# Tiles 64 bytes further on: where TensorE's two operands lie in a transformer block

## The chip, the cores and the metric

One core of a Trainium2 chip runs the whole program. The metric is the device time of one execution in microseconds (us); the figure for a kernel is the median of its runs.

## The reference

The kernel computes one block over 256 tokens of width 2048 in float32: a wide input projection, two branches (a gated delta rule with short convolutions, and a sparse attention that picks 64 keys per query), a gated merge, and a feed-forward part of width 5632, with two layer norms. Cut to its large products:

```python
proj = x @ w_in[l]                                   # 2048 -> 11864 columns
...
merged = jax.nn.sigmoid(gate_a) * (o_a @ w_branch_a[l]) + jax.nn.sigmoid(gate_b) * (o_b @ w_branch_b[l])
x = layer_norm(DEEPNORM_ALPHA * x + merged @ w_out[l], ln1_g[l], ln1_b[l])
h_gate, h_up = jnp.split(x @ w_ffn_in[l], 2, axis=-1)
x = layer_norm(DEEPNORM_ALPHA * x + (jax.nn.silu(h_gate) * h_up) @ w_ffn_out[l], ln2_g[l], ln2_b[l])
```

## The kernel before

Every large product is made of three products in TensorE's float32r type: each factor is split into a part that this type holds (`hi`) and the rest (`lo`), and hi·hi, hi·lo and lo·hi are summed in PSUM.

Weights come in chunks of 128 × 1024 float32. The helper `chunk` (L65) takes a buffer `raw`, loads it by a DMA from the SP queue, casts it on ScalarE into `hi` (L72) and subtracts on VectorE into `lo` (L74). `raw`, `hi` and `lo` lie in the pool `wp`, which has four buffers of each; consecutive chunks use them in turn.

Two helpers then multiply. In `group_ws` (L123) the weights are the stationary operand, those that lie still in TensorE, and the activations move: for each of four blocks of 128 rows and each of two blocks of 128 columns, the hi block meets 512 columns of an `X2` tile (both parts of the activations, side by side; L134), and the lo block meets 256 columns, their hi part alone (L136). Such a pair of matmuls is the unit of the text. 62 groups of 4 chunks of 8 pairs make 1984 pairs: 20 groups (640 pairs) in the first stage, up to about 293 us, and 42 (1344 pairs) for the feed-forward input, from 788 to 1264 us. In `xs_mm` (L146) it is the other way round: an activation block of 128 × 128 is the stationary operand and the weight chunk moves, 512 columns a matmul, three matmuls for hi·hi (L153), lo (L154) and the activations' lo part (L155). The activations are `X2` in the projections to gates and values, in `wo` and in the first feed-forward block, `oh_` and `ol_` in the two branch products, and `hH`/`hL` in the last product. In `block_xs_stag` four chunks of a block are kept in an extra pool (`ex`), not in `wp`.

`ws_mm` (L107), of the first block, has weights stationary and 256 columns moving; it is called for the four column blocks of `win` chunks and once more for the small weights in `oh_`/`ol_` (L117, L119, L120).

The order of TensorE and SP is that of the program text (`manual_schedule`); smaller products of the two branches are slipped in between chunks by `tick()`.

**Where the tiles lie.** A partition is filled from the left in the order of the pools: `cst`, `wp`, `sm`, then the tiles of the first phase (`p1`), which later give way to `x1`, `hH`, `hL` and the extra pools; `X2` lies at the right end, behind it only the small tile `pad`. Every tile starts on a multiple of 32 bytes. The starts in bytes of a partition, before the change:

| tile | start | start modulo 256 |
|---|---|---|
| `raw`, 4 buffers | 17024 + 4096 i | 128 |
| `hi`, 4 buffers | 33408 + 4096 i | 128 |
| `lo`, 4 buffers | 49792 + 4096 i | 128 |
| `warm` and the other small tiles (`sm`) | 66176 | |
| first tile of `p1`, later `x1` | 66624 | 64 |
| `hH`, `hL` | 83008 and on, steps of 4096 | 64 |
| `oh_`, `ol_` | 156736, 164928 | 64 |
| `hi`, `lo` of the extra pools | 140352 and on | 64 |
| `X2`, 4 tiles | 196480 + 8192 i | 128 |

A stationary block takes 512 bytes of a partition, and blocks follow each other at multiples of 512 bytes; a moving operand of 512 columns takes 2048 bytes.

Of the kernel before, what the change touches and what calls it, by code (L numbers as in the profile page):

```python
# [8 lines left out]
F32 = mybir.dt.float32  # L9
F32R = mybir.dt.float32r  # L10
# [7 lines left out]
P = 128  # L18
# [14 lines left out]
LEAD = 70  # L33
LN1_AHEAD = ((20, 20, 20), (38, 32, 22))
X1T_WAIT = (4, 5)
INV_WAIT = 6
VT_WAIT = 6
N_WARM = 9

C_ID, C_TRI, C_ONE, C_M1, C_M2, C_M3, C_LV, C_SH = 0, 128, 256, 384, 512, 640, 768, 960  # L40
# [4 lines left out]
def block_kernel(ctx: ExitStack, tc: tile.TileContext, xT, x, cpack, onehot, relb, convw, alog, dtb, gnw,  # L45
                 ws, wws, win, wba, wbb, wo, wfi, wfg, wfo, ln1g, ln1b, ln2g, ln2b, out):
    nc = tc.nc

    cst = ctx.enter_context(tc.tile_pool(name="cst", bufs=1, side="left"))
    wp = ctx.enter_context(tc.tile_pool(name="wp", bufs=4, side="left"))  # L50
    sm = ctx.enter_context(tc.tile_pool(name="sm", bufs=1, side="left"))
# [4 lines left out]
    def ps_aux():  # L56
        return aux.tile([P, 512], F32, name="aux", tag="aux")

    def ps_acc():
        return acc.tile([P, 512], F32, name="acc", tag="acc")  # L60
# [1 line left out]
    ident = cst.tile([P, P], F32, name="ident")  # L62
    ctx.enter_context(tc.manual_schedule(engines={mybir.EngineType.PE, mybir.EngineType.SP}))

    def chunk(src, pool=None, lead=LEAD):  # L65
        n = src.shape[1]
        pool = pool or wp
        with tc.high_priority(offset=lead):
            raw = wp.tile([P, n], F32, name="raw", tag="raw")
            nc.sync.dma_start(raw, src)  # L70
            hi = pool.tile([P, n], F32R, name="hi", tag="hi")
            nc.scalar.copy(hi, raw)  # L72
            lo = pool.tile([P, n], F32R, name="lo", tag="lo")
            nc.vector.tensor_sub(lo, raw, hi.bitcast(F32))  # L74
        return hi, lo

# [7 lines left out]
    def tick():  # L84
        clock[0] += 1
        for ch in list(chains):
            wait = ch[1]
            if isinstance(wait, str):
                if wait not in done or done[wait] >= clock[0]:
                    continue  # L90
            elif wait > clock[0]:
                continue
            try:
                n = next(ch[0])
            except StopIteration:
                chains.remove(ch)
                continue
            ch[1] = n if isinstance(n, str) else clock[0] + n
# [24 lines left out]
    def group_ws(srcs):  # L123

        pss = [ps_acc(), ps_acc()]
        for ci, src in enumerate(srcs):
            hi, lo = chunk(src)
            hv = hi.rearrange("p (k c) -> p k c", k=4)
            lv = lo.rearrange("p (k c) -> p k c", k=4)
            for kk in range(4):  # L130
                k = 4 * ci + kk
                for c in range(2):
                    cs = slice(c * P, (c + 1) * P)
                    nc.tensor.matmul(pss[c], hv[:, kk, cs], X2[k // 4][:, k % 4], start=(k == 0), stop=False,  # L134
                                     skip_group_check=True)
                    nc.tensor.matmul(pss[c][:, :S], lv[:, kk, cs], xh[:, k, :], start=False, stop=(k == KT - 1),  # L136
                                     skip_group_check=True)
            tick()
        return pss
# [17 lines left out]
    def block_xs(srcs, lh, ll):  # L157
        pss = [ps_acc(), ps_acc()]
        for ci, src in enumerate(srcs):
            hi, lo = chunk(src)  # L160
            for tb in range(NTB):
                xs_mm(pss[tb], hi, lo, ci, len(srcs), lh, ll, tb)
            tick()
        return pss

    def block_xs_stag(srcs, lh, ll, extra, after):

        pss = [ps_acc(), ps_acc()]
        n = len(srcs)
        held = []  # L170
        for ci, src in enumerate(srcs):
            hi, lo = chunk(src, extra if n - 8 <= ci < n - 4 else None)
            xs_mm(pss[0], hi, lo, ci, n, lh, ll, 0)
            if ci < n - 8:
                xs_mm(pss[1], hi, lo, ci, n, lh, ll, 1)
            else:
                held.append((ci, hi, lo))
            tick()
        after(0, pss[0])
        for ci, hi, lo in held:  # L180
            xs_mm(pss[1], hi, lo, ci, n, lh, ll, 1)
            tick()
        after(1, pss[1])
# [8 lines left out]
    padp = ctx.enter_context(tc.tile_pool(name="padp", bufs=1, side="right"))  # L192
    pad = padp.tile([P, 24], F32, name="pad")
    nc.vector.memset(pad, 0.0)
    xs_ = ExitStack()
    xpool = xs_.enter_context(tc.tile_pool(name="xp", bufs=1, side="right"))
    X2 = [xpool.tile([P, KT // 4, 2, S], F32R, name=f"X2_{i}") for i in range(4)]
# [58 lines left out]
    def groups(chain, ev, *args):  # L256

        for c in (0, 2):
            b = gidx[0]
            gidx[0] += 1  # L260
            start(chain(c, group_ws([wws[b, k] for k in range(4)]), ev if c else None, *args))
# [22 lines left out]
    a = ps_aux()  # L284
    for _ in range(N_WARM):
        nc.tensor.matmul(a[:, :P], s_bm[:, 0, :P], s_bm[:, 0, P:], start=True, stop=True)
# [3 lines left out]
    for i in range(8):  # L290
        k0 = 2 * i
        parts = [srcs[i]] if i > 2 else [srcs[i][:, :512], srcs[i][:, 512:]]
        for j, src in enumerate(parts):
            k, n = k0 + j, 2 // len(parts)
# [3 lines left out]
            hi, lo = chunk(src, lead=0)  # L298
# [289 lines left out]
    def value_chain():  # L588
        for h0, ev in ((0, "vc0"), (4, "vc1")):
            yield ev  # L590
            yield VT_WAIT
            for tb in range(NTB):
# [368 lines left out]
    for f in range(2, FT):  # L961
        start(f_chain(f, group_ws([wfg[f - 2, k] for k in range(4)])))
# [115 lines left out]
```

## Time and profile before

| | us |
|---|---|
| median of 3 runs | 1511.9 |
| the runs | 1511.41, 1511.9, 1519.5 |
| the profiled execution, its own time | 1518.93 |
| its span, first to last instruction | 1517.2 |
| TensorE (PE) matmuls busy | 1502.1 (99%) |
| weight loads (PEld) busy | 1277.3 (84%) |
| VectorE (DVE) busy | 904.8 (60%) |
| ScalarE (ACT) busy | 696.1 (46%) |

PE is TensorE's matmuls and PEld its weight loads, which run beside them. A matmul's busy time includes the time in which its results drain; the next one starts before that ends, so busy times of PE overlap, and the distance between starts is what adds up to the span.

### The profile page before, as it was taken

The numbers are of one execution on the slowest core, as the hardware profiler recorded it, in microseconds if no ns is written. First come the engines' busy times: TensorE is split into PE (matmuls) and PEld (weight loads), VectorE is DVE, ScalarE is ACT, GpSimd is POOL, SyncE is SP. The second block draws the span as 40 slices with busy tenths as digits, with TensorE's granted clock in tenths as the row PEclk, the third lists the DMA queues.
The fourth block names the chain that finished last, engine by engine and source line by source line (L and its number), as shares of the span: only waits on it lengthen the run. The fifth ranks groups of instructions, "written<-read, shape, count | busy, mean of one in ns | idle before, by whom it ended". The sixth has DMA issues, their size and how long they took to land.

```text
span 1517.2 us, 20367 instructions
## 1 busy us (share of the span) xinstructions
PE 1502.1 (99%) x7920; PEld 1277.3 (84%) x7920; DVE 904.8 (60%) x1237; ACT 696.1 (46%) x914; POOL 40.2 (3%) x40
## 2 busy tenths in 40 slices
PE   9999999999999999999999999999999999999997
PEld 8888888888888888888888888888888888888885
DVE  6798984465464554565675555555555555545455
ACT  6765443445544344443444444444444444333341
POOL 0011010020100000000000000000000000000000
PEclk9999999999999999999999999999999999999999
DMA  8646574434465555558545555555555556555562
GB/s 295 188 154 201 173 188 153 153 125 167 153 219 194 190 188 193 190 182 296 194 158 190 186 189 183 191 182 188 187 183 192 181 190 241 193 194 192 189 207 92
DMA packets 86352, 284.59 MB, mean 188 GB/s; under 512 B 15776, under 2 KB 16840, under 8 KB 85488
## 3 DMA queue, kind: packets, MB, share of 16 engines
q1 hardware_dynamic: 77856, 273.39, 54.6%
q0 software_dynamic: 1360, 7.54, 1.7%
q10 hardware_dynamic: 7040, 2.36, 0.7%
q8 instruction: 62, 1.02, 0.3%
q14 instruction: 34, 0.28, 0.0%
HBM read 280.44 MB, written 2.82 MB: 187 GB/s over the span
## 4 chain that ended last, share of the span: by engine, by line
PE 97%; DMA 1%; DVE 1%; ACT 0%; issue 0%; SPq 0%; POOLq 0%; DVEq 0%; ACTq 0%
PE acc L134 31%; PE acc L153 15%; PE acc L136 15%; PE acc L155 15%; PE acc L154 15%; PE aux L585 1%; DMA raw<-in_win_dram 1%; PE aux L800 0%; PE aux L739 0%; PE aux L479 0%; PE aux L454 0%; PE aux L566 0%; PE aux L499 0%; ACT hi L72 0%; PE aux L651 0%; DVE lo L74 0%
## 5 line engine op out<-in xcount | busy, mean ns | idle before, releaser
L74 DVE TENSOR_TENSOR lo<-raw,hi 128x1024 fp32r<-128x1024 f32 (+1 forms) x515 | 632.4, 1230 | 509.1 <-ACT hi L72 508.1
L72 ACT CAST hi<-raw 128x1024 fp32r<-128x1024 f32 (+1 forms) x515 | 538.2, 1046 | 654.1 <-PE acc L155 353.9
L134 PE MATMUL acc<-X,hi 128*128 128x512 f32 x1984 | 703.3, 399 | 0.0
L136 PE MATMUL acc<-X,lo 128*128 128x256 f32 x1984 | 556.1, 280 | 0.0
L134 PEld LDWEIGHTS acc<-X,hi 128*128 128x128 f32 x1984 | 372.7, 188 | 92.3 <-issue 1.0
L136 PEld LDWEIGHTS acc<-X,lo 128*128 128x128 f32 x1984 | 374.5, 189 | 0.0
L153 PE MATMUL acc<-hi,X 128*128 128x512 f32 x544 | 214.6, 394 | 0.0
L155 PE MATMUL acc<-hi,X 128*128 128x512 f32 x544 | 212.1, 390 | 0.0
L154 PE MATMUL acc<-lo,X 128*128 128x512 f32 x544 | 211.9, 390 | 0.0
L153 PE MATMUL acc<-hi,hH 128*128 128x512 f32 x352 | 138.7, 394 | 0.0
L155 PE MATMUL acc<-hi,hL 128*128 128x512 f32 x352 | 138.0, 392 | 0.0
L154 PE MATMUL acc<-lo,hH 128*128 128x512 f32 x352 | 136.6, 388 | 0.0
L155 PEld LDWEIGHTS acc<-hi,X 128*128 128x128 f32 x544 | 102.1, 188 | 21.6
L154 PEld LDWEIGHTS acc<-lo,X 128*128 128x128 f32 x544 | 102.2, 188 | 20.6
L153 PEld LDWEIGHTS acc<-hi,X 128*128 128x128 f32 x544 | 102.2, 188 | 20.6
L155 PEld LDWEIGHTS acc<-hi,hL 128*128 128x128 f32 x352 | 66.1, 188 | 15.4
L154 PEld LDWEIGHTS acc<-lo,hH 128*128 128x128 f32 x352 | 66.1, 188 | 14.7
L153 PEld LDWEIGHTS acc<-hi,hH 128*128 128x128 f32 x352 | 66.2, 188 | 13.2
L953 ACT COPY ft<-acc 128x256 f32<-128x256 f32 x84 | 31.0, 369 | 62.6 <-PE acc L136 62.6
L954 DVE TENSOR_TENSOR ft<-acc,ft 128x256 f32<-128x256 f32 x84 | 35.4, 421 | 26.7 <-ACT ft L953 26.7
L153 PE MATMUL acc<-hi,oh__102 128*128 128x512 f32 x128 | 50.7, 396 | 0.0
L154 PE MATMUL acc<-lo,oh__102 128*128 128x512 f32 x128 | 50.3, 393 | 0.0
(268 smaller groups left out, 864.0 us busy)
## 6 DMA issues: line engine op xcount, KB each, us to landing
raw<-in_wfg_dram SPq DMA_DIRECT2D x168, 512.0 KB, 3.3
raw<-in_win_dram SPq DMA_DIRECT2D x101, 512.0 KB, 3.3
raw<-in_wfo_dram SPq DMA_DIRECT2D x88, 512.0 KB, 3.3
raw<-in_wws_dram SPq DMA_DIRECT2D x80, 512.0 KB, 3.4
raw<-in_wo_dram SPq DMA_DIRECT2D x32, 512.0 KB, 4.4
raw<-in_wbb_dram SPq DMA_DIRECT2D x16, 512.0 KB, 3.3
raw<-in_wba_dram SPq DMA_DIRECT2D x16, 512.0 KB, 3.3
raw<-in_wfi_dram SPq DMA_DIRECT2D x8, 512.0 KB, 4.4
```

The lines of the kernel that those rows point to most:

```text
L72: nc.scalar.copy(hi, raw)
L74: nc.vector.tensor_sub(lo, raw, hi.bitcast(F32))
L134: nc.tensor.matmul(pss[c], hv[:, kk, cs], X2[k // 4][:, k % 4], start=(k == 0), stop=False, skip_group_check=True)
L136: nc.tensor.matmul(pss[c][:, :S], lv[:, kk, cs], xh[:, k, :], start=False, stop=(k == KT - 1), skip_group_check=True)
L153: nc.tensor.matmul(ps, xh, hv[:, kk], start=(k == 0), stop=False)
L154: nc.tensor.matmul(ps, xh, lv[:, kk], start=False, stop=False)
L155: nc.tensor.matmul(ps, xl, hv[:, kk], start=False, stop=(k == 2 * n - 1))
L585: nc.tensor.matmul(o, l, r, start=True, stop=True)
L953: nc.scalar.copy(t[:, i], ps[:, S:])
L954: nc.vector.tensor_add(t[:, i], ps[:, :S], t[:, i])
```

## The change

The hi and lo tiles of the pool `wp` grow by 32 elements (128 bytes). A chunk is put `at` elements into its tile: 16 (64 bytes) where `group_ws` asks for it, 0 elsewhere. A new tile `pads` of 64 bytes, set to zero and read by nobody, is the first of the pool `sm`, which follows `wp`.

```diff
+WS_AT = 16
...
-    def chunk(src, pool=None, lead=LEAD):
+    def chunk(src, pool=None, lead=LEAD, at=0):
...
             raw = wp.tile([P, n], F32, name="raw", tag="raw")
             nc.sync.dma_start(raw, src)
-            hi = pool.tile([P, n], F32R, name="hi", tag="hi")
+            hi = pool.tile([P, n + (2 * WS_AT if pool is wp else 0)], F32R, name="hi", tag="hi")[:, at:at + n]
             nc.scalar.copy(hi, raw)
-            lo = pool.tile([P, n], F32R, name="lo", tag="lo")
+            lo = pool.tile([P, n + (2 * WS_AT if pool is wp else 0)], F32R, name="lo", tag="lo")[:, at:at + n]
             nc.vector.tensor_sub(lo, raw, hi.bitcast(F32))
...
         for ci, src in enumerate(srcs):
-            hi, lo = chunk(src)
+            hi, lo = chunk(src, at=WS_AT)
...
     nc.vector.memset(pad, 0.0)
+    pads = sm.tile([P, 16], F32, name="pads")
+    nc.vector.memset(pads, 0.0)
```

The buffers of `hi` then start at 33408 + 4224 i and those of `lo` at 50304 + 4224 i, both at 128, 0, 128, 0 modulo 256; the weights of `group_ws` begin 64 bytes later, at 192, 64, 192, 64. All that lies behind `wp` on the left moves by 1024 + 64 = 1088 bytes: `hH`, `hL`, `oh_`, `ol_` and the extra pools' chunks then start at 128 modulo 256. `raw` and `X2` stay where they were.

## Rows read from the trace of the kernel before

**Rows 1.** The page's busy table, and the mean granted clock of the core.

```profile
PE 1502.1 (99%) x7920; PEld 1277.3 (84%) x7920; DVE 904.8 (60%) x1237; ACT 696.1 (46%) x914; POOL 40.2 (3%) x40
...
core 0: 1517.2 us, clock 0.998
```

**Rows 2.** The page's chain that ended last, by engine and by line.

```profile
PE 97%; DMA 1%; DVE 1%; ACT 0%; issue 0%; SPq 0%; POOLq 0%; DVEq 0%; ACTq 0%
PE acc L134 31%; PE acc L153 15%; PE acc L136 15%; PE acc L155 15%; PE acc L154 15%; PE aux L585 1%; DMA raw<-in_win_dram 1%; PE aux L800 0%; PE aux L739 0%; PE aux L479 0%; PE aux L454 0%; PE aux L566 0%; PE aux L499 0%; ACT hi L72 0%; PE aux L651 0%; DVE lo L74 0%
```

**Rows 3.** The page's groups: count, busy us, mean ns, idle before.

```profile
L74 DVE TENSOR_TENSOR lo<-raw,hi 128x1024 fp32r<-128x1024 f32 (+1 forms) x515 | 632.4, 1230 | 509.1 <-ACT hi L72 508.1
L72 ACT CAST hi<-raw 128x1024 fp32r<-128x1024 f32 (+1 forms) x515 | 538.2, 1046 | 654.1 <-PE acc L155 353.9
L134 PE MATMUL acc<-X,hi 128*128 128x512 f32 x1984 | 703.3, 399 | 0.0
L136 PE MATMUL acc<-X,lo 128*128 128x256 f32 x1984 | 556.1, 280 | 0.0
...
L153 PE MATMUL acc<-hi,X 128*128 128x512 f32 x544 | 214.6, 394 | 0.0
...
L153 PE MATMUL acc<-hi,hH 128*128 128x512 f32 x352 | 138.7, 394 | 0.0
...
L153 PE MATMUL acc<-hi,oh__102 128*128 128x512 f32 x128 | 50.7, 396 | 0.0
```

**Rows 4.** Windows, 787 to 1265 us: length, busy us (count) per engine, clock, DMA.

```profile
787.00:1265.00 478.00, 478.00 (x2704) 414.53 (x2703) 272.04 (x338) 227.66 (x339) 1.11 (x2) 1.00 0.57 188
```

**Rows 5.** Timeline (start us, us, engine, line), long stage: pairs 1 and 7.

```profile
899.94 0.40 PE L134 MATMUL acc<-X,hi 128*128 128x512 f32 x1
...
902.06 0.40 PE L134 MATMUL acc<-X,hi 128*128 128x512 f32 x1
```

**Rows 6.** Timeline of TensorE, first stage: pairs 1 and 13.

```profile
274.81 0.40 PE L134 MATMUL acc<-X,hi 128*128 128x512 f32 x1
...
278.97 0.40 PE L134 MATMUL acc<-X,hi 128*128 128x512 f32 x1
```

**Rows 7.** Timeline of TensorE, `ws_mm`: matmuls 1 and 13 of each run.

```profile
25.68 0.28 PE L117 MATMUL acc<-X,hi 128*128 128x256 f32 x1
...
27.12 0.28 PE L117 MATMUL acc<-X,hi 128*128 128x256 f32 x1
...
27.48 0.28 PE L117 MATMUL aux<-X,oh__102 128*128 128x256 f32 x1
...
28.84 0.28 PE L117 MATMUL acc<-X,hi 128*128 128x256 f32 x1
```

**Rows 8.** Timeline of TensorE, `xs_mm` over `X2`: matmuls 1 and 31.

```profile
450.11 0.39 PE L153 MATMUL acc<-hi,X 128*128 128x512 f32 x1
...
456.91 0.39 PE L153 MATMUL acc<-hi,X 128*128 128x512 f32 x1
```

**Rows 9.** Timeline of TensorE, `xs_mm` over `oh_`, `hH`: matmuls 1 and 31.

```profile
499.81 0.39 PE L153 MATMUL acc<-hi,oh__102 128*128 128x512 f32 x1
...
506.68 0.39 PE L153 MATMUL acc<-hi,oh__102 128*128 128x512 f32 x1
...
1300.27 0.39 PE L153 MATMUL acc<-hi,hH 128*128 128x512 f32 x1
...
1307.14 0.39 PE L153 MATMUL acc<-hi,hH 128*128 128x512 f32 x1
```

**Rows 10.** Timeline of TensorE, chunks in the extra pool: matmuls 1 and 10.

```profile
742.87 0.39 PE L153 MATMUL acc<-hi,X 128*128 128x512 f32 x1
...
744.97 0.39 PE L153 MATMUL acc<-hi,X 128*128 128x512 f32 x1
```

**Rows 11.** Start: `pad`'s memset (timeline), first chunk's load (chain).

```profile
0.80 0.08 DVE L194 MEMSET pad<- 128x24 f32 x1 [0.80 <-PEq L1068]
...
3.06 4.85 DMA raw<-in_win_dram
```

## The prediction

> **What bounds the kernel.** I read the busy shares first [rows 1]: TensorE is busy 99% of the span and its clock is at the 2.4 GHz level throughout (granted clock 0.998). The chain that ended last says the same: 97% of it is TensorE, and five matmul lines carry 91% [rows 2]. A change that moves no bytes and adds no matmul can only matter through the distance from one matmul's start to the next. That distance is not in the groups' means (394 to 399 ns for 512 columns [rows 3]): those include the drain, which overlaps the next matmul. I take it from start times in the timeline, over many matmuls at once.
>
> For the pairs of `group_ws` (512 columns under a hi weight block, then 256 under a lo block) six pairs take 902.06 − 899.94 = 2.12 us, 353.3 ns a pair [rows 5]; the whole stage of 42 groups agrees, as 42 × 32 = 1344 pairs fill about 475 of its 478 us [rows 4]. At the end of the first stage the same pair, at the same addresses, takes 4.16 / 12 = 346.7 ns [rows 6]: there are two rhythms, and a stage can hold either.
>
> Now the same shapes by where the operands lie. I write "distance" for the address of the weights being loaded for the next matmul minus that of the moving operand, modulo 256 bytes; it follows from the table of addresses, and every step inside a tile is a multiple of 512 bytes.
> - 256 columns, distance 0: 1.44 / 12 = 120.0 ns. Distance 192 (stationary operand 64 past a multiple of 128, moving operand on one): 1.36 / 12 = 113.3 ns [rows 7].
> - 512 columns, distance 0: 6.80 / 30 = 226.7 ns [rows 8]. Distance 192: 6.87 / 30 = 229.0 ns, both with `oh_` and with `hH` [rows 9]. Distance 64 (here the moving operand is the one off the multiple of 128): 2.10 / 9 = 233.3 ns [rows 10].
>
> So the placement of the two operands TensorE reads at one time does set its pace, by up to 7 ns a matmul. The short rhythm of a pair is just the two rows of distance 0 added, 226.7 + 120.0 = 346.7; the long one has 6.6 ns more.
>
> The Trainium skill speaks against all this: "TensorE: Matmul & The Clock Gate", section "Step-by-step: what each phase is for", says that weights are loaded through a read port of their own and take nothing from the running matmul, and "SBUF — State Buffer", section "SBUF: two separate sides", that TensorE waits for nobody. By the first page's warm gap (512 / 2.4 + 2.5) a 512-column matmul would be 215.8 ns wherever its operands lie, and the change would do nothing. The trace disagrees: 226.7, 229.0 and 233.3 ns at one shape and one clock.
>
> **The change, part by part.** The profiled execution took 1518.9 us, 7.0 above the median of 1511.9. That is about what 1344 pairs differ by between the two rhythms (6.6 × 1344 = 8.9 us; the three runs lie 8.1 apart), so I read it as a run whose long stage fell into the long rhythm.
>
> 1. *Weights 64 bytes into their tiles.* The moving X2 stays on a multiple of 128 and the weights are 64 past one. The rows nearest in kind (stationary off, moving on) are 113.3 ns for 256 columns and 229.0 for 512, together 342.3. In the long stage that saves 353.3 − 342.3 = 11.0 ns × 1344 = 14.8 us. In the first stage the 640 pairs lie between 346.7 and 353.3; I take 350, which saves 7.7 × 640 = 4.9 us. Bounds for the pair: nothing seen is under 113.3 + 226.7 = 340.0, and 120.0 + 233.3 + 6.6 = 360 has all that rows show against it.
> 2. *The 1088 bytes behind the weight buffers* (8 × 128 + 64). `hH`, `hL`, `oh_`, `ol_` go from 64 past a multiple of 128 onto one, so `xs_mm` meets the case of [rows 8]: 229.0 − 226.7 = 2.3 ns on 3 × (352 + 128) = 1440 matmuls [rows 3], less 48 whose chunks lie in the extra pool at distance 0 already, 3.2 us saved. The chunks kept in the extra pools move by 1088 as well: 233.3 − 226.7 = 6.6 ns on 96 matmuls (two staged blocks over X2, four chunks each), 0.6 us saved. The 48 matmuls of the small weights lose what they had, +6.7 ns, 0.3 us. Tiles of the chains move together and keep their distances to one another.
> 3. *The cast and the subtraction* write 64 bytes further on, same shape and count: 1046 and 1230 ns [rows 3]. No row shows such a write; between no cost and a tenth more (0.1 us of each) nothing shows, since a chunk of `group_ws` lasts 8 × 353 = 2.8 us and ACT and DVE stand idle 654 and 509 us before these very lines. Without that cover 248 chunks × 0.1 would be 25 us. The loads into `raw` keep their addresses.
> 4. *The new memset* is like that of `pad`, 0.08 us of DVE, while the first weight chunk is still to land (4.85 us from 3.06) [rows 11]; uncovered it would be 0.08 us.
>
> Sum: 1518.9 − 14.8 − 4.9 − 3.2 − 0.6 + 0.3 = 1495.7, say **1496 us**. It starts from the profiled execution, but each term replaces a pace by a pace, so it doesn't depend on which rhythm a run of before had. Were the new pair to have a long rhythm too, 6.6 × 1344 = 8.9 us come back: 1504.6.
>
> **The rivals.**
>
> *The pace goes by 256 bytes, and half the buffers land wrong.* The tiles grow by 128, so the four buffers of hi and lo alternate: their starts modulo 256 are 128, 0, 128, 0, and the shifted weights lie at distance 64, 192, 64, 192 from X2. For it: distances 64 and 192 differ in the trace (233.3 against 229.0), although they are the same modulo 128. Against it: those two also differ in which operand is off the multiple of 128, and distance 64 with the stationary one off is in no row. Then half the pairs are 342.3, the other half 233.3 + 113.3 to 126.6 = 346.6 to 359.9; mean about 347.8. The moving chunks of `xs_mm` alternate as well, and half of them are 128 from the stationary operand, which no row shows; I take 231.1, midway between 64 and 192 (bounds 226.7 and 233.3). Over X2 that is +4.4 ns × 768 = +3.4 us; over `hH` and `oh_` half gain 2.3 and half lose 2.1, about zero. Time: 1518.9 − 5.5 × 1344 / 1000 − 2.2 × 640 / 1000 + 3.4 − 0.6 + 0.3 = **1513 us** (1505 to 1521), no change that can be told.
>
> *Slower, by the same alternation at its dear end.* The place is `group_ws` in buffers 0 and 2. If a pair there takes 359.9 and the others carry the 6.6 ns of a long rhythm (348.9), the mean is 354.4; against the short rhythm that I read into the median that is 7.7 × 1344 = 10.3 us, and 4.4 × 640 = 2.8 us in the first stage. With 233.3 at distance 128, `xs_mm` adds 6.6 × 768 = 5.1 and, over `hH` and `oh_`, (4.3 − 2.3) × 720 = 1.4 us. Time: 1511.9 + 19.6 = **1531 us**. It decides from a mean pair over about 349 ns with distance 128 at 231 or dearer. For it: the rhythm of long stages is the long one in this profile. Against: it needs both the 256 rule and the top of each bound.
>
> *The change does nothing.* The pair may be held by something that the addresses don't move, and only part 2 remains: about **1508 us** in the profile's terms of a short rhythm (1511.9 − 3.6). For it: the individual starts wander (the two rhythms) at fixed addresses. Against: 113.3 against 120.0, next to each other, same shape [rows 7]. The skill's rule above ends here too, with 1511.9 by its own gap.
>
> **How the numbers follow.** The forecast 0.42, the 256 rule without net effect 0.33, nothing 0.10, slower 0.15. Half a per cent, 7.6 us, is about what a measurement of this kernel tells from no change. Faster (under 1504.3): 0.40 of the forecast and 0.05 of the second case, 0.45. Slower (over 1519.5): 0.15 and 0.04, 0.19. The rest, 0.36, is the same. The range starts below the forecast, with the pair at 340.0 (1984 × 2.3 = 4.6 us less, 1491, and a little for the first stage's mean, 1490), and reaches over the second case to 1521; beyond lies most of the slower case, some 0.15. The forecast's own range is 1490 to 1505.
>
> **What would show it.** Right: in the changed profile the starts of `group_ws` pairs lie 342 ns apart in every chunk, `xs_mm` over `hH` and `oh_` runs at 226.7 ns as over X2, and the counts, the casts and the loads are as before. The 256 rule: the pair's distance changes from chunk to chunk, every second one dearer, and `xs_mm` alternates as well. Nothing: 346.7 or 353.3 in all chunks. It goes wrong if distance 64 with the stationary operand off is dear, if 128 is dear, or if a new long rhythm holds the pair.

## The result: 1527.4 us, slower

| kernel | median us | its runs |
|---|---|---|
| before | 1511.66 | six, 1510.5 to 1520.29 |
| after | 1527.36 | six, 1526.88 to 1527.97 |

The ratio is 1.0074, 95% interval 1.0047 to 1.0101: slower by some 0.7%, where 1496 was forecast. The runs of before lie at two times, near 1510.5 and near 1519.5, with none between 1512.5 and 1518.2 in 29 runs on one chip; those of after lie at one.

The page after: busy table, chain, groups (columns as in [rows 1 to 3]).

```profile
PE 1510.6 (99%) x7920; PEld 1280.7 (84%) x7920; DVE 905.0 (59%) x1238; ACT 695.5 (46%) x914; POOL 40.2 (3%) x40
...
PE 97%; DMA 2%; DVE 0%; SPq 0%; issue 0%; ACT 0%; POOLq 0%; DVEq 0%; ACTq 0%
...
L76 DVE TENSOR_TENSOR lo<-raw,hi 128x1024 fp32r<-128x1024 f32 (+1 forms) x515 | 632.3, 1229 | 514.2 <-ACT hi L74 513.1
L74 ACT CAST hi<-raw 128x1024 fp32r<-128x1024 f32 (+1 forms) x515 | 536.7, 1043 | 660.3 <-PE acc L157 363.1
L136 PE MATMUL acc<-X,hi 128*128 128x512 f32 x1984 | 704.4, 398 | 0.0
L138 PE MATMUL acc<-X,lo 128*128 128x256 f32 x1984 | 558.6, 282 | 0.0
...
L155 PE MATMUL acc<-hi,X 128*128 128x512 f32 x544 | 215.9, 397 | 0.0
...
L155 PE MATMUL acc<-hi,hH 128*128 128x512 f32 x352 | 138.0, 392 | 0.0
```

Behind the loads of the start nothing moved but the pace of TensorE: its clock is as before (0.998), the chain is 97% TensorE again, the counts are the same, and cast and subtraction take 1043 and 1229 ns against 1046 and 1230 [rows 3]. The groups hide the loss: the hi matmuls of `xs_mm` over `X2` are a little dearer (397 against 394), over `hH` a little cheaper (392 against 394). It shows in the starts. (Two lines were added above: L134, L136 and L153 of before are L136, L138 and L155 here.)

Timeline of TensorE after: start us, us, engine, line.

```profile
797.08 0.39 PE L136 MATMUL acc<-X,hi 128*128 128x512 f32 x1
...
899.27 0.40 PE L136 MATMUL acc<-X,hi 128*128 128x512 f32 x1
...
901.39 0.40 PE L136 MATMUL acc<-X,hi 128*128 128x512 f32 x1
...
902.44 0.40 PE L136 MATMUL acc<-X,hi 128*128 128x512 f32 x1
...
904.21 0.40 PE L136 MATMUL acc<-X,hi 128*128 128x512 f32 x1
...
1302.04 0.39 PE L155 MATMUL acc<-hi,hH 128*128 128x512 f32 x1
...
1302.74 0.39 PE L155 MATMUL acc<-hi,hH 128*128 128x512 f32 x1
...
1304.78 0.40 PE L155 MATMUL acc<-hi,hH 128*128 128x512 f32 x1
...
1307.57 0.39 PE L155 MATMUL acc<-hi,hH 128*128 128x512 f32 x1
...
1310.30 0.40 PE L155 MATMUL acc<-hi,hH 128*128 128x512 f32 x1
```

- *Pairs.* In a chunk at distance 192 six pairs take 901.39 − 899.27 = 2.12 us, 353.3 ns each; in the next chunk, at 64, five take 1.77 us, 354 by these rounded starts. Both are at the pace of the long rhythm of before [rows 5]. No group of the long stage runs faster: with the change of place between chunks counted in, each pair takes 352.9.
- *`xs_mm`.* Of the last five rows, four are the starts of successive chunks of twelve matmuls, at distances 0, 128, 0 and 128 (1302.74 is the fourth matmul of the first): 2.74, 2.79 and 2.73 us. Once settled, nine matmuls at distance 0 take 2.04 us, 226.7 ns; at 128 the starts lie 229 and 237.5 ns apart in turn, 233.3. The first three matmuls of a chunk at 0 still come 0.70 us apart, not 0.68: changing places costs a little too. Before, all were at 229.0 [rows 9].
- *Where the time came from.* From start to start in the two profiled executions: first pair 1.4 us later (37.76 against 36.39; the other profiles gave 36.2 to 38.9), the first stage 262.1 against 260.4, from it to the long stage 497.23 against 491.96, the long stage 474.5 against 475.1, the last product 242.8 against 241.5. That is 1.4 + 1.7 + 5.3 − 0.6 + 1.3 = 9.1, and 1518.9 + 9.1 = 1528.0; the profiled execution took 1527.97. The 1.4 us are the loads of the start: the last one in the chain (start us, us; first after, then before) lands at 28.27 us, before at 26.96. That the change has a part in this isn't shown.

```profile
23.16 5.11 DMA raw<-in_win_dram
...
22.07 4.89 DMA raw<-in_win_dram
```

### The profile page after: what moved, and what is told of

Its sections match the earlier page's. It is cut to its first block, busy times and chain, and to the rows that moved or that the text cites. A ratio compares the mean times of both kernels' runs of the same rounds, so it can differ in the third digit from the quotient of the medians.

```text
span 1526.1 us, 20368 instructions
## 1 busy us (share of the span) xinstructions
PE 1510.6 (99%) x7920; PEld 1280.7 (84%) x7920; DVE 905.0 (59%) x1238; ACT 695.5 (46%) x914; POOL 40.2 (3%) x40
## 4 chain that ended last, share of the span: by engine, by line
PE 97%; DMA 2%; DVE 0%; SPq 0%; issue 0%; ACT 0%; POOLq 0%; DVEq 0%; ACTq 0%
PE acc L136 31%; PE acc L138 16%; PE acc L157 15%; PE acc L155 15%; PE acc L156 15%; PE aux L589 1%; DMA raw<-in_win_dram 1%; DMA cp<-in_cpack_dram 1%; PE aux L804 0%; PE aux L743 0%; PE aux L483 0%; PE aux L458 0%; PE aux L570 0%; PE aux L503 0%; PE aux L655 0%; PE aux L469 0%
## 5 line engine op out<-in xcount | busy, mean ns | idle before, releaser
L76 DVE TENSOR_TENSOR lo<-raw,hi 128x1024 fp32r<-128x1024 f32 (+1 forms) x515 | 632.3, 1229 | 514.2 <-ACT hi L74 513.1
L74 ACT CAST hi<-raw 128x1024 fp32r<-128x1024 f32 (+1 forms) x515 | 536.7, 1043 | 660.3 <-PE acc L157 363.1
L136 PE MATMUL acc<-X,hi 128*128 128x512 f32 x1984 | 704.4, 398 | 0.0
L138 PE MATMUL acc<-X,lo 128*128 128x256 f32 x1984 | 558.6, 282 | 0.0
L136 PEld LDWEIGHTS acc<-X,hi 128*128 128x128 f32 x1984 | 373.0, 188 | 90.6 <-issue 1.0
L138 PEld LDWEIGHTS acc<-X,lo 128*128 128x128 f32 x1984 | 373.0, 188 | 0.0
L155 PE MATMUL acc<-hi,X 128*128 128x512 f32 x544 | 215.9, 397 | 0.0
L155 PE MATMUL acc<-hi,hH 128*128 128x512 f32 x352 | 138.0, 392 | 0.0
L155 PEld LDWEIGHTS acc<-hi,X 128*128 128x128 f32 x544 | 102.2, 188 | 22.0
L155 PEld LDWEIGHTS acc<-hi,hH 128*128 128x128 f32 x352 | 66.1, 188 | 14.9
L155 PE MATMUL acc<-hi,oh__104 128*128 128x512 f32 x128 | 50.7, 396 | 0.0
L157 PE MATMUL acc<-hi,ol__105 128*128 128x512 f32 x128 | 50.3, 393 | 0.0
```

The source lines that it names most:

```text
L155: nc.tensor.matmul(ps, xh, hv[:, kk], start=(k == 0), stop=False)
L157: nc.tensor.matmul(ps, xl, hv[:, kk], start=False, stop=(k == 2 * n - 1))
```

## The experiments

I call (hi, lo) a *place*: by how much the hi and the lo weights of `group_ws` lie past the X2 tile, modulo 256 bytes. The 512 columns of a pair run beside the load of the lo weights, the 256 columns beside that of the next hi weights: in the kernel before, the hi matmul that starts at 902.06 us [rows 5] and the lo matmul that starts at 902.29 us each start with a load (timeline of the weight loads):

```profile
902.06 0.19 PEld L136 LDWEIGHTS acc<-X,lo 128*128 128x128 f32 x1
902.29 0.19 PEld L134 LDWEIGHTS acc<-X,hi 128*128 128x128 f32 x1
```

Before is (0, 0); after is (64, 64) and (192, 192) in turn. Each interval is for the ratio to runs of before on the same chip.

**1. The 64 bytes behind the buffers alone.**

```diff
 (against the kernel before)
+    pads = sm.tile([P, 16], F32, name="pads")
+    nc.vector.memset(pads, 0.0)
```

> Only the 64-byte tile: the tiles do not grow and no chunk is shifted, so hH, hL, oh_, ol_ and the extra pools' chunks move by 64 bytes, onto the same place modulo 256 as hi, lo and X2 (distance 0 everywhere). Theory A, that the pace of TensorE goes by the distance of its two operands modulo 256 bytes: xs_mm over hH and oh_ falls from 229.0 to 226.7 ns a matmul, the extra pools' chunks from 233.3 to 226.7, group_ws keeps 346.7 or 353.3; 3 to 4 us less than before in the same rhythm. Rival B, that moving the tiles behind the weight buffers is itself what costs: xs_mm or the chains get dearer, and the time goes up towards 1520 us even where group_ws is in its short rhythm.

Measured: 1516.26 us (1515.0 to 1518.38), ratio 0.9989 (0.9971 to 1.0006). Timeline, matmuls 1 and 31 over `hH`:

```profile
1300.01 0.39 PE L153 MATMUL acc<-hi,hH 128*128 128x512 f32 x1
...
1306.81 0.39 PE L153 MATMUL acc<-hi,hH 128*128 128x512 f32 x1
```

6.80 / 30 = 226.7 ns: `hH` off its 64 runs as X2 does. This part of the sum holds, where the moving chunks stay in place. The long stage ran at 353.2 ns a pair, so the time belongs beside the 1519.5 of before: about 3 us, as costed. All twelve runs lie at this one time, though the pairs stand at the place where before's have two.

**2. The larger tiles without the shift.**

```diff
 (against the changed kernel)
-            hi, lo = chunk(src, at=WS_AT)
+            hi, lo = chunk(src)
```

> The changed kernel with the shift of group_ws taken back (its chunks begin at 0): tiles still grow by 128, so the four buffers alternate between distance 0 and 128. Theory A: xs_mm is as in the changed kernel, 226.7 ns in every second chunk and 233.3 in the others, which holds some 8 to 10 us of the change's loss; group_ws has 346.7 to 353.3 at distance 0 and an unknown pace at 128. Between 1517 and 1528 us. Rival C, that the shifted weights of group_ws hold the whole loss: back to 1512 or less.

Measured: 1521.26 us (1520.18 to 1523.48), ratio 1.0023 (1.0005 to 1.0041). Timeline: the start of the long stage, then of three successive chunks of twelve matmuls over `hH`, at 0, 128 and 0:

```profile
794.67 0.40 PE L136 MATMUL acc<-X,hi 128*128 128x512 f32 x1
...
1295.21 0.39 PE L155 MATMUL acc<-hi,hH 128*128 128x512 f32 x1
...
1297.95 0.40 PE L155 MATMUL acc<-hi,hH 128*128 128x512 f32 x1
...
1300.74 0.39 PE L155 MATMUL acc<-hi,hH 128*128 128x512 f32 x1
```

`xs_mm` alternates as after: 232.6 ns a matmul at 128, 228.1 at 0, the change of place counted in (2.79 and 2.74 us a chunk). The long stage starts at 794.67 us, 5.9 later than in before's profile, with no 64-byte shift anywhere, and its pairs, at (0, 0) and (128, 128) in turn, take 349.6. So the growth alone brings the loss in `xs_mm`, and the shift adds 6.1 us, mostly by holding the long stage at 353 (474.5 us against 470.1 here).

**3 and 9. Tiles that grow by 256, so that all buffers agree.** Everything of `group_ws` at 192, or at 64; `xs_mm` at 0 in every chunk.

```diff
 (against the changed kernel; hi and lo alike)
-            hi = pool.tile([P, n + (2 * WS_AT if pool is wp else 0)], ...)
+            hi = pool.tile([P, n + (64 if pool is wp else 0)], ...)
...
-WS_AT = 16
+WS_AT = 48    # the run at 192; 16 in the run at 64
...
-    tab = T("tab", [H, 384])
+    tab = s_u.rearrange("p a d -> p (a d)")[:H, :384]
```

> The changed kernel with tiles that grow by 256 instead of 128, so that all buffers lie alike, and the shift of group_ws at 192 bytes: distance 192 in all pairs, distance 0 in all of xs_mm. (tab takes its room from s_u for this.) The forecast's step, that a pair is the sum of its two rows at distance 192 (113.3 and 229.0): 342.3 ns a pair, 1496 us. Theory A, by the changed kernel's odd buffers: 353.3 ns a pair, xs_mm at 226.7 ns everywhere; 1515 to 1517 us.

> As the changed kernel, but the weight tiles grow by 256 bytes instead of 128 (and the 384-column table lies in the space of a scratch tile to make room), so every buffer keeps its place by 256: group_ws stands at distance 64 in every chunk, xs_mm at distance 0 in every chunk. If the loss of the change is the half of xs_mm that it puts at distance 128, then xs_mm goes back to 226.7 to 227 ns, the stage of the 42 last groups stays at 353 ns a pair, its start falls back from 797.1 us to within 2 us of 789, and the time is 1515 to 1519.5 us. If the loss came from group_ws at 64 or 192 itself, or from the larger tiles, the time stays at 1524 to 1528 us.

Measured at 192: 1517.25 us, ratio 0.9992 (0.997 to 1.0015); four runs at 1512.0 to 1512.3, six at 1517.1 to 1518.1. At 64: 1518.26 us (1517.23 to 1519.01), ratio 0.9998 (0.9987 to 1.001). Timeline of the run at 192, pairs 1 and 15:

```profile
899.58 0.39 PE L136 MATMUL acc<-X,hi 128*128 128x512 f32 x1
...
904.46 0.39 PE L136 MATMUL acc<-X,hi 128*128 128x512 f32 x1
```

Timeline of the run at 64, the start of the long stage, then pairs 1 and 13 of a group:

```profile
790.71 0.40 PE L136 MATMUL acc<-X,hi 128*128 128x512 f32 x1
...
899.74 0.40 PE L136 MATMUL acc<-X,hi 128*128 128x512 f32 x1
...
903.98 0.40 PE L136 MATMUL acc<-X,hi 128*128 128x512 f32 x1
```

4.88 / 14 = 348.6 and 4.24 / 12 = 353.3: the forecast's 342.3 is at neither place. At 64 the stage starts 6.4 us earlier than after and the run is 9.1 us shorter, with the pairs alike. So the half of `xs_mm` at distance 128 is what parts these two kernels: from the first stage to the long one after takes 497.2 us against 490.9 here, in the last product 242.8 against 239.2, together 10.0 us. Against before, whose `hH` and `oh_` lie at 192, the same stretches lost 6.6 us.

**4. A map of places.** One execution; the tiles as above, another place for each group of the long stage and another distance for each block of `xs_mm`.

```diff
+            hi, lo = chunk(src, dh=dh, dl=dl)    # places of this group
```

> A map in one run. Tiles grow by 256 and each chunk is put where a table says. The 42 groups of the long stage go through all 16 pairs of distances (hi, lo) from 0, 64, 128, 192, then ten equal finer ones (16, 32, 48, 240, 224, 208, 8, 248, 96, 160), then the 16 again; the 26 blocks of xs_mm that block_xs makes go through distances from 0 to 252. Theory A: a matmul of 512 columns runs at 226.7, 233.3, 233.3 and 229.0 ns at 0, 64, 128 and 192; finer steps show whether the pace changes in jumps or evenly. If hi and lo act each on its own (the 512-column matmul by lo's distance, the 256-column one by hi's), lo at 0 with hi at 192 gives 226.7 + 113.3 = 340 ns a pair; if the pair is locked as a whole, it stays at 346.7 or 353.3 in all 16. The time as a whole says little: 1515 to 1530 us.

Pairs, ns, pairs 5 to 29 of a group; each place stood twice and gave the same within 0.3 (but (0, 0): 352.3 over the first 14 pairs of the stage, and 346.7 the second time):

| hi \ lo | 0 | 64 | 128 | 192 |
|---|---|---|---|---|
| 0 | 346.7 to 352.3 | 346.7 | 346.7 | 350.0 |
| 64 | 340.0 | 353.3 | 350.0 | 353.3 |
| 128 | 351.8 | 346.7 | 351.1 | 346.7 |
| 192 | 340.0 | 346.7 | 346.7 | 353.3 |

`xs_mm`, 512 columns: 226.7 at distance 0, 228.9 at 4, 232 to 234 at 8, 239.5 at 12, 236.7 at 16, 230.0 at 48, 233.3 at 64, 232.4 at 128, 228.9 at 192, 237.2 at 252. Timeline of the map, `xs_mm` at distance 12, matmuls 1 and 10, then a group at (64, 0), pairs 1 and 13 (L170 and L151 are the hi lines here):

```profile
524.78 0.40 PE L170 MATMUL acc<-hi,oh__104 128*128 128x512 f32 x1
...
526.94 0.40 PE L170 MATMUL acc<-hi,oh__104 128*128 128x512 f32 x1
...
846.19 0.39 PE L151 MATMUL acc<-X,hi 128*128 128x512 f32 x1
...
850.27 0.39 PE L151 MATMUL acc<-X,hi 128*128 128x512 f32 x1
```

2.16 / 9 = 240 ns and 4.08 / 12 = 340.0. The fastest places, (64, 0) and (192, 0), take what the two fastest rows of one shape add up to, 226.7 + 113.3. Hi and lo both at 64 or both at 192 are among the dearest here, and (64, 192) with them. Equal distances alone are not what costs: ten finer places with hi and lo at one distance, each once, gave 346.7 at 16, 32, 48, 96 and 224, 348.9 at 8, 350.0 at 160 and 208, 351.7 at 248 and 353.3 at 240. For `xs_mm` no distance tried is as good as 0.

**5 and 6. Hi alone, lo alone.**

```diff
 (against the kernel before, with `pads`; the run with lo alone does the same to lo)
-            hi = pool.tile([P, n], F32R, name="hi", tag="hi")
+            hi = pool.tile([P, n + (4 * WS_AT if pool is wp else 0)], F32R, name="hi", tag="hi")[:, at:at + n]
```

> The changed kernel with the hi tiles alone grown, by 256, and the hi chunks of group_ws alone shifted, by 64; lo keeps its place, so that all of lo and all of xs_mm lie at distance 0. Theory A in the form that the map gave it: a matmul's pace goes by the distance of the weights that are loaded while it runs, those of the next matmul, so the 512-column matmul goes by lo (0: 226.7) and the 256-column one by hi (64: 113.3). 340.0 ns in every pair, 13.3 us... per thousand pairs less than the long rhythm of before; 1518.9 - 17.9 (long stage) - 6.4 (first stage) - 3.8 (xs_mm) = 1491 us, without two rhythms. Rival D, that the pace goes by the place of a matmul's own weights: the 512-column matmul has the shifted block (233), the 256-column one is at 120, 353 ns a pair, 1515 us.

> The same the other way round: lo alone grown by 256 and shifted by 64. Theory A: the 512-column matmul, which loads lo, gets dearer (229 to 231), the 256-column one stays near 117; 346.7 ns a pair as the map has it for hi 0, lo 64; 1518.9 - 8.9 - 2.1 - 3.8 = 1504 us. Rival D, own weights: 226.7 + 113.3 = 340 ns, 1491 us.

Measured, hi alone: 1510.3 us (1509.45 to 1512.15), ratio 0.9956 (0.9937 to 0.9974). Lo alone: 1505.48 us (1504.88 to 1506.18), ratio 0.9923 (0.9892 to 0.9954). Timeline with hi alone, pairs 1 and 13 in the first and in the long stage:

```profile
61.23 0.39 PE L136 MATMUL acc<-X,hi 128*128 128x512 f32 x1
...
65.31 0.39 PE L136 MATMUL acc<-X,hi 128*128 128x512 f32 x1
...
899.74 0.39 PE L136 MATMUL acc<-X,hi 128*128 128x512 f32 x1
...
903.94 0.39 PE L136 MATMUL acc<-X,hi 128*128 128x512 f32 x1
```

And with lo alone, pairs 1 and 13:

```profile
899.51 0.39 PE L136 MATMUL acc<-X,hi 128*128 128x512 f32 x1
...
903.67 0.39 PE L136 MATMUL acc<-X,hi 128*128 128x512 f32 x1
```

Lo alone gives 4.16 / 12 = 346.7, and so in the whole long stage, as expected. Hi alone missed: at one and the same place the first rows give 340.0 and the last 350.0. A place allows several rhythms; a map read as one pace for each place was too simple. The rival D of the two expectations, that a matmul goes by its own weights, called for 353 ns a pair with hi alone and 340 with lo alone; the long stages show 350.0 and 346.7.

**7. The other operand moved.** The kernel before with X2 64 bytes further left; one execution.

```diff
-    pad = padp.tile([P, 24], F32, name="pad")
+    pad = padp.tile([P, 40], F32, name="pad")
```

> The kernel before with the small tile behind X2 made 64 bytes larger, so that X2 moves by 64 bytes to the left and nothing else moves. If only the distance counts: group_ws at distance 64 in all pairs, 353.3 ns and the sequence 235, 118 of the changed kernel's even buffers; xs_mm over X2 at distance 192, 229.0 instead of 226.7; over hH and oh_ unchanged at 229.0; the extra pools' chunks over X2 at distance 0, 226.7 instead of 233.3. About 1518.9 + 3.5 = 1522 us. If the address of the weights counts by itself, all paces stay as before.

Measured: 1524.02 us. Timeline, pairs 1 and 13:

```profile
899.74 0.40 PE L134 MATMUL acc<-X,hi 128*128 128x512 f32 x1
...
903.98 0.40 PE L134 MATMUL acc<-X,hi 128*128 128x512 f32 x1
```

353.3 as at (64, 64) after, with starts 235 and 118 ns apart there too, and `xs_mm` over X2, at 192 now, takes 229.0. It is the difference of the two addresses that counts, not which operand is off a multiple of 128.

**8. A second map**, one execution, same tiles and edit: lo at 0 with hi at each multiple of 16, then hi at 192 with lo so, then twelve single places.

> A second map: xs_mm at distance 0 everywhere; in the long stage hi goes through 16 to 240 in steps of 16 with lo at 0, then lo the same way with hi at 192, then single finer ones. Theory A: lo at 0 keeps the 512-column matmul at 226.7 whatever hi is, and hi at 64 and 192 gives 113.3; it does not say what lies between; a value of hi under 113.3 would give a version under 340 ns. With hi at 192, lo off 0 costs 2 to 7 ns or more.

Measured: 1509.49 us. With lo at 0, the fifteen places of hi took 344.4 to 352.6; (64, 0) and (192, 0), 340.0 in the first map, took 350.0. With hi at 192, only (192, 16) took 340.0, the others 346.2 to 353.3. Of the single places, 346.2 to 353.3 as well, four with lo at 0 stood a second time: (176, 0) took 351.7 and then 346.5, the other three the same within 0.8.

**10. The place (192, 16) everywhere.**

```diff
 (against the run at 64; hi likewise, with 3 * at)
-...  name="lo", tag="lo")[:, at:at + n]
+...  name="lo", tag="lo")[:, at // 4:at // 4 + n]
```

> Tiles as in the run with everything at distance 64, but the hi chunks of group_ws stand at 192 and the lo chunks at 16, the place where the second map saw 340.0 ns a pair in one group; xs_mm stays at 0. If the distance fixes the pace, all groups of the last stage take 340.0 ns a pair, 6.7 ns below the run with lo alone at 64, and the time is 1505.5 - 6.7 ns x 1984 pairs = 1492 us. If how the stage is entered decides as much as the distance, the pace falls to another rhythm of 346.7 or 350.0 ns somewhere in the stage and the time is 1503 to 1511 us.

Measured: 1513.21 us, ratio 0.9928 (0.9893 to 0.9962); three runs at 1495.9 to 1496.8, seven at 1512.5 to 1514.5. The profiled one, 1495.91, has 340.0 in every group of the long stage but the first. The gap of about 17 us is 13.3 × 1344 = 17.9, so the others should be runs at 353.3; of those there is no profile. In the profiled run the rhythm changes inside the first group of the long stage (pairs 9 and 24, two small matmuls of another product, pairs 27 and 32):

```profile
788.54 0.40 PE L136 MATMUL acc<-X,hi 128*128 128x512 f32 x1
...
793.84 0.40 PE L136 MATMUL acc<-X,hi 128*128 128x512 f32 x1
...
794.19 0.38 PE L944 MATMUL aux<-ident,sg 128*128 128x128 f32 x2
...
795.09 0.39 PE L136 MATMUL acc<-X,hi 128*128 128x512 f32 x1
...
796.79 0.39 PE L136 MATMUL acc<-X,hi 128*128 128x512 f32 x1
```

5.30 / 15 = 353.3 ahead of the two and 1.70 / 5 = 340.0 behind them. The same two matmuls turn the run with hi alone from 340.0 to 350.0. In the profiles of the kernels that keep one place throughout, a pace changes only where matmuls of another product have come in between, never in the 1320 pairs of the long stage behind these two. The next run shows both rhythms in one, at a change of place.

**11. The same place behind different neighbours**, one execution.

```diff
+CAND = [(192, 16), (192, 0), (64, 0), (208, 16), (176, 16), (192, 24), (200, 16), (0, 192), (64, 16), (192, 240)]
+FEED = [x for c in CAND for x in ((64, 64), c, (0, 64), c)] + [(0, 64), (192, 16)]
```

> The last stage again as a map, tiles with 256 bytes more: ten places (hi, lo), each set once behind a group at (64, 64), which runs at 353.3 ns a pair, and once behind a group at (0, 64), which runs at 346.7; the first stage stands at (0, 64), xs_mm at 0. The places are (192,16), (192,0), (64,0), (208,16), (176,16), (192,24), (200,16), (0,192), (64,16), (192,240). Theory H: the pace of a group is one of 340.0, 346.7 and 353.3 ns (or an average of two), and the group before decides which of those that its place allows it takes; then (192,16), (192,0) and (64,0) give 340.0 behind one neighbour and 346.7 to 353.3 behind the other, and at least three of the ten places differ between their two turns by 3 ns or more. Theory D: the place alone decides, and each place gives the same pace in both turns within 1 ns; then (192,16) gives 340.0 twice, and the seven slower runs of the kernel with (192,16) everywhere lost their time elsewhere.

Measured: 1508.61 us. Timeline, (192, 16) behind (64, 64), then behind (0, 64), pairs 1 and 13 of each (L149 is the hi line):

```profile
801.01 0.40 PE L149 MATMUL acc<-X,hi 128*128 128x512 f32 x1
...
805.25 0.40 PE L149 MATMUL acc<-X,hi 128*128 128x512 f32 x1
...
823.33 0.39 PE L149 MATMUL acc<-X,hi 128*128 128x512 f32 x1
...
827.41 0.39 PE L149 MATMUL acc<-X,hi 128*128 128x512 f32 x1
```

353.3, then 340.0, with the same addresses. (192, 0) took 350.0 and 340.2, (176, 16) 352.8 and 346.6, (64, 16) 346.8 and 340.0; (0, 192) 350.2 and 351.4; the other five agreed within 0.3. (64, 0), which I had expected to differ, took 350.0 twice, and a third group at (192, 16), behind (0, 64) again, took 353.3; there the second 512-column matmul took 0.26 us (starts at 1244.94 and 1245.20 us). The entry has a say, but not by the pace of the neighbour alone.

**12. The place (64, 16) everywhere**, which never took more than 346.8.

```diff
 (against the run of 10)
-...  name="hi", tag="hi")[:, 3 * at:3 * at + n]
+...  name="hi", tag="hi")[:, at:at + n]
```

> As the run with hi at 192 and lo at 16, but hi at 64: in the map of entries this place gave 346.8 ns a pair behind one neighbour and 340.0 behind the other, never 353.3. If both are steady rhythms and the entry picks one, every run lies at one of two times, 1495 to 1497 us (340.0 in the last stage) or 1503 to 1506 us (346.7), none at 1513. If 346.8 was only the start of a change to 340.0, all runs lie at 1495 to 1497 us. If the place falls back to 353.3 as the one with 192 did, some lie at 1512 to 1515 us. With lo alone at 64 the time was 1505.5 us; a median under 1504 beats it.

Measured: 1493.69 us, ratio 0.9844 (0.9811 to 0.9877), the fastest kernel of the study; four runs, 1493.38 to 1496.42, none near 1503. Timeline, pairs 1 and 13:

```profile
899.62 0.39 PE L136 MATMUL acc<-X,hi 128*128 128x512 f32 x1
...
903.70 0.39 PE L136 MATMUL acc<-X,hi 128*128 128x512 f32 x1
```

340.0, and so in all groups of the long stage after its first; the first stage has stretches of 340.0 and of 346.7, and `xs_mm` stands at 226.7 to 227.1 in nearly all chunks. Whether a longer series would also show the 346.7 rhythm in the long stage, four runs can't say.

## Why the prediction was wrong

- *"The rows nearest in kind ... are 113.3 ns for 256 columns and 229.0 for 512, together 342.3."* This step failed, and with it 14.8 + 4.9 us of the sum. Its first fault is the kind: I sorted rows by which operand is off a multiple of 128. Experiment 7 moves the other operand and gives the same 353.3: only the difference counts, modulo 256. The second is the addition: the rows come from streams of one shape, and a pair of two shapes need not be their sum. At 192, where both rows were read, the pairs of one run take 353.3 in the first stage and 348.6 in the long one, there about 230 for the 512 columns and about 119, not 113.3, for the 256; no run holds 342.3. The long stage gave back 0.6 us instead of 14.8, the first cost 1.7 instead of saving 4.9.
- *Part 2, 3.2 us saved by `hH` and `oh_` on a multiple of 128.* Right for the 64 bytes alone (experiment 1). But the tiles grow by 128 and the moving chunks alternate by 128, so half these matmuls pay 233.3: the last product lost 1.3 us. Between the two stages, mostly over X2, the same half added 5.3 us, a term that the forecast's sum left out. Of the 32 us between the sum and the profiled execution, 14.2 are the long stage's, 6.6 the first's, 10.1 those of `xs_mm` and the small weights (3.5 forecast as saved, 6.6 lost) and 1.4 the start's.
- *The 256 rule* was the right mechanism, in the two rivals where I had put it. "I take 231.1, midway", was too low for distance 128: 233.3 at steady pace, the upper bound. With it the slower rival's terms for `xs_mm`, 5.1 and 1.4 us, come close to what was measured, 5.3 and 1.3. Its mean pair, 354.4, came out as 353, but by another way: not 359.9 and 348.9 in turn, but 353.3 at both places. So that its 1531 lies only 3.6 us too high is partly luck.
- *Two rhythms, and the profiled run in the long one*: borne out as far as profiles go. One place shows two paces in one execution (experiments 5 and 11). That a kernel's two times are its two rhythms fits their distance (8.9 us forecast, 9 measured), but no run of before at 1510.5 has a profile. "Were the new pair to have a long rhythm too" named the danger, at 8.9 us; the changed kernel shows no other in its long stage (one profile, and six runs within 1.1 us of each other). Against the faster runs of before the loss is therefore 1527.4 − 1510.5 = 17 us, against the others 8.
- *Parts 3 and 4, casts and memset at nothing*: right, as the groups after show.
- The Trainium skill's rule weighed in the prediction ("TensorE: Matmul & The Clock Gate", section "Step-by-step: what each phase is for": the load of weights takes nothing from the running matmul) does not hold here: one matmul of 512 columns takes 226.7 to 239.5 ns by the distance of the weights being loaded beside it, and never 215.8. That figure is an estimate by the gap that the same section of the Trainium skill gives, 512 / 2.4 + 2.5.

Open: how an interruption or a change of place picks a rhythm, and why (64, 64) showed only the long one wherever it stood, while (192, 192) has both 348.6 and 353.3. The runs show that it is so, not by what part of the chip.

## What to carry to other kernels

Where TensorE is the bound, take the distance from start to start and sort it by the difference between the moving operand's address and that of the weights being loaded beside it, modulo 256 bytes; size each tile so that all buffers of a pool keep that difference, or one edit becomes two. Don't count on the sum of paces from streams of one shape to forecast a mixed one (it held in one rhythm of (192, 0), not at (192, 192)): run a map with another place for each group, which costs one execution, and then time the best place everywhere, since a place can have several rhythms. When a kernel's runs fall at two times, compare its profile only with runs at that same time.

## What was not expected of the hardware

- The pace of a pair moves in steps: 340.0, 346.7 and 353.3 ns, 6.7 apart (16 cycles at 2.4 GHz), and means between them such as 348.9 and 350.0. The best and the worst differ by 13.3 ns, 3.9%, at equal work and granted clock.
- One place can hold either of two rhythms: (192, 16) kept 353.3 through a group of 32 pairs in one turn and 340.0 in another, and two small matmuls of another product in between were enough to change it.
- Distances of a few bytes matter: 226.7 ns at 0, 228.9 at 4, 239.5 at 12.
